# Hybrid decoder layer on one core: the whole value projection first, LRU gates and scans in the key and query steps

## The chip, the cores and the metric

The kernel runs on one core of one Trainium2 chip. The metric is the device time of one execution in microseconds, as a median of several runs. Engines are named as in the profile: PE is TensorE (PEld its weight loads), DVE is VectorE, ACT is ScalarE, POOL is GpSimd, SP is SyncE, which issues most of the DMAs.

## What is computed

One layer of a hybrid decoder on x of 256 tokens by 2048 channels, all in float32:

```python
u = rmsnorm(h, ln1_w)
proj = u @ w_in                      # six parts of 1024: lru_x, lru_g, q, k, v, ret_g
lru_x = causal_depthwise_conv(lru_x, conv_w, conv_b)
y_lru = rg_lru(lru_x, ...) * gelu(lru_g)        # two 128-wide gates per block, then a scan over the tokens
y_ret = retention(q, k, v, ret_g, gn_w)         # 8 heads, rotary, decay, group norm, swish gate
h = h + concat(y_lru, y_ret) @ w_out
u = rmsnorm(h, ln2_w)
h = h + (silu(u @ w_ffn_gate) * (u @ w_ffn_up)) @ w_ffn_down
return rmsnorm(h, final_norm_w)
```

The scale of the first rmsnorm is not applied to u. The kernel multiplies x by ln1_w alone and scales the results of the projections by 1/rms of the token; that factor comes from the sum of squares over all 2048 channels.

## The kernel before

**Precision.** Each float32 operand is split in two parts, a rounded high part h (a cast on ACT, L101) and the rest l (a subtraction on DVE, L102). A product is then three matmuls: h by h, h by l, l by h. Weights pass through the same split as they arrive: `Unit.load` (L111) takes 1024 columns of a weight into a `raw` buffer (five of them), casts into `wh` and subtracts into `wl` (four of each). In the value projection at the start this is done in two pieces of 512 columns.

**Order of the work.** All PE work is a list of steps, `program`. At the end of the function (L949 to L963) a loop goes through it: it issues the loads that a step needs and three more (`AHEAD = 3`), then the step's matmuls, and then calls `tick`, which runs what was put off with `defer(n, f)` n steps before. The order in which the program hands out instructions is their priority; a planner at compile time then fixes the order of each engine's queue and lets work whose operands are ready move ahead into gaps. At run time each queue is in order.

**Two kinds of step.** `fm_tile` (L165) gives a tile with the channels on partitions: 16 steps of k, each with one matmul of 512 columns (L140) and one of 256 (L141). `tm_block` (L180) gives a block with the tokens on partitions: four k's per weight unit, two token tiles, three matmuls of 512 columns (L156 to L158). A matmul of either kind fills a PSUM bank; there are four in the pool `bank` and four in `aux`. The `halfway` list is looked at in the middle of an `fm_tile`, at n == 8: there the norm's small products go in.

**The steps before the change.** First the left 512 columns of the value projection (`v0`, four steps), while x arrives (`load_x`, L858) and `make_u` (L275) turns it into u. `v0_out` (L870) copies the results out of PSUM unscaled, asks for the identity matrix and calls `squares` (L284): eight squares on ACT, the adds on POOL. The sum goes through `rms_scale` (L246): two small products on PE (L250), a reciprocal square root on DVE, two diagonal tiles (L254), and in the middle of the next tile a product that spreads it over the partitions (L260). `then` (L880) scales the two value tiles on POOL. Next are eight lru_x tiles (`lru_in` behind each: convolution on DVE), eight key tiles, eight query tiles (`qk_half`: rotary), the right 512 columns of the value projection (four steps), eight steps of the retention gate, which start with one head each (`head`), and eight lru gate tiles. Behind them come the output projection, the feed-forward part and the last norm, which the change doesn't touch.

The gates of the LRU (`lru_gate`, L354: six matmuls each), their roots (`lru_roots`, L370) and the scans (`lru_scan`, L375: a reciprocal, the scan instruction and six more on DVE, one square on ACT) are put off from the lru_x tiles. Before, the first four gates come behind the fourth key tile, the roots behind the first query tile, the scans from the third query tile to the seventh step of the retention gate. They have to be done when `lru_out` (L391) uses them.

Of the kernel before, what the change touches and what calls it, by code (L numbers as in the profile page):

```python
# [10 lines left out]
AF = mybir.ActivationFunctionType  # L11
ALU = mybir.AluOpType
# [24 lines left out]
def tile_hymba_layer(ctx: ExitStack, tc: tile.TileContext, A: dict, out: bass.AP):  # L37
# [21 lines left out]
    def act_tile(name, dt=F32):  # L59
        return apool.tile([P, 512], dt, tag="act", name=nm(name))  # L60
# [158 lines left out]
    def defer(steps, f):  # L219
        later.append([steps, f])  # L220
# [54 lines left out]
    def make_u(k):  # L275
        hl = act_tile("u", F32R)
        act.activation(out=hl[:, :S], in_=xs(k), func=AF.Copy, scale=col(C_LN1 + k))  # L277
        v.scalar_tensor_tensor(
            out=hl[:, S:], in0=xs(k), scalar=col(C_LN1 + k), in1=hl[:, :S].bitcast(F32),
            op0=ALU.mult, op1=ALU.subtract,  # L280
        )
        u[k] = hl

    def squares():  # L284
        for i in range(KT // 2):
            sq = act_tile("sq") if i else sumsq
            act.activation(out=sq, in_=xt[i], func=AF.Square)
            if i:
                pool.tensor_tensor(out=sumsq, in0=sumsq, in1=sq, op=ALU.add)
        pool.tensor_tensor(out=sumsq[:, :S], in0=sumsq[:, :S], in1=sumsq[:, S:], op=ALU.add)  # L290


    gw = [None] * 4
# [149 lines left out]
    def v_out(c, t, ps):  # L443
        vv[2 * t + c] = act_tile("v")
        act.activation(out=vv[2 * t + c], in_=ps, func=AF.Copy, scale=r1_tok[:, t : t + 1])
# [412 lines left out]
    def load_x(k):  # L858
        if k == 0:
            nc.sync.dma_start(out=small, in_=A["small"])  # L860
        if k < 2:
            nc.sync.dma_start(out=xt[0][:, k * S : k * S + S], in_=A["x"][0][:, k * S : k * S + S])
        elif k % 2 == 0:
            nc.sync.dma_start(out=xt[k // 2], in_=A["x"][k // 2])

    v0 = [
        Unit(A["w_v"][i], 2, lambda k, i=i: load_x(4 * i + k), lambda k, i=i: make_u(4 * i + k)) for i in range(4)
    ]

    def v0_out(t, ps, c0, cw):  # L870
        vv[2 * t] = act_tile("v")
        act.copy(out=vv[2 * t], in_=ps)
        if t == 0:
            return
        nc.sync.dma_start(out=ident, in_=A["ident"])
        squares()
        defer(2, load_gates)
        defer(3, lambda: halfway.append(lambda: rms_scale(sumsq[:, :S], r1_tok, r1, then)))

    def then():  # L880
        for t in range(2):
            pool.tensor_scalar(out=vv[2 * t], in0=vv[2 * t], scalar1=r1_tok[:, t : t + 1], scalar2=None, op0=ALU.mult)
        defer(2, lru_decay)
        trig[0] = act_tile("trig")
        nc.sync.dma_start(out=trig[0], in_=A["trig"])

    tm_block(v0, lambda k: u[k], v0_out)

    for n in range(NLRU):

        def post(ps, n=n):
            defer(max(1, 4 - n), lambda: lru_in(n, ps))
            defer(max(9, 12 - n), lambda: lru_gate(n))
            if n == NLRU - 1:
                defer(10, lru_roots)
                for m in range(NLRU):
                    defer((12, 15, 18, 20, 22, 24, 26, 28)[m], lambda m=m: lru_scan(m))

        fm_tile(Unit(A["w_lx"][n]), u, range(KT), post, room=aux if n in (2, 3, 6, 7) else bank)

    first = [True]
    for which in ("k", "q"):
        for j in range(4):
            for e in range(2):
# [7 lines left out]
                    qk_half(which, j, e, ps)  # L912

                fm_tile(Unit(A["w_" + which][2 * j + e]), u, range(KT), post)

    tm_block([Unit(A["w_v"][4 + i]) for i in range(4)], lambda k: u[k], lambda t, ps, c0, cw: v_out(1, t, ps))

    for c in range(2):

# [144 lines left out]
```

## Time and profile before

| | us |
|---|---|
| median of three runs | 1105.15 (1104.84 to 1106.02) |
| the profiled execution, its own time | 1106.04 |
| its span, first to last instruction | 1103.3 |
| PE busy | 1092.4 (99%) |
| DVE busy | 885.3 (80%) |
| ACT busy | 622.1 (56%) |
| POOL busy | 57.9 (5%) |

The profile is of one execution; its span leaves out what lies before the first instruction and behind the last. A row of a timeline gives the start, the time, engine, line, operation, tiles and count; with a count of two or more, the time is that of the group from its first start to its last end. Matmuls overlap: one of 512 columns has a length of 0.39 us, but the next one starts 0.23 us after it. The square bracket at the end says how long the engine was idle before and what ended that. A row of windows gives the stretch, its length and the busy time of each engine.

### The profile page before, as it was taken

How to read it: one execution, taken by the hardware profiler on the slowest of the kernel's cores; microseconds unless marked ns; L12 is line 12 of the kernel's file. 1: busy time of each engine (PE TensorE's matmuls, PEld its weight loads, DVE VectorE, ACT ScalarE, POOL GpSimd, SP SyncE). 2: the span in 40 equal slices, each digit the busy share in tenths (PEclk: the TensorE clock that was granted, in tenths of full speed). 3: DMA queues.
4: the chain of work that ended last, by engine and by line, in shares of the span. 5: the costliest groups of instructions: out<-in, count | busy, mean ns of one | idle time of the engine just before them, and what ended most of it. 6: DMA issues, size and time to landing. Idle time of an engine off the chain costs nothing.

```text
span 1103.3 us, 14624 instructions
## 1 busy us (share of the span) xinstructions
PE 1092.4 (99%) x5328; PEld 920.5 (83%) x5328; DVE 885.3 (80%) x1249; ACT 622.1 (56%) x846; POOL 57.9 (5%) x64
## 2 busy tenths in 40 slices
PE   9999999999999999999999999999999999999996
PEld 7888888888888988888888888888888888888885
DVE  7798799978776787788787878877887999777874
ACT  7666644468665665554554545544545675554552
POOL 0602130000000000000000000000000000020001
PEclk9999999999999999999999999999999999999999
DMA  9765575554665465645746646556456465646562
GB/s 329 239 199 168 171 245 170 176 188 143 194 220 187 155 207 174 213 154 186 247 132 214 226 156 229 187 191 219 159 195 234 153 219 196 224 161 218 201 230 76
DMA packets 62215, 214.71 MB, mean 195 GB/s; under 512 B 7104, under 2 KB 7488, under 8 KB 62144
## 3 DMA queue, kind: packets, MB, share of 16 engines
q1 hardware_dynamic: 61344, 211.70, 57.6%
q0 software_dynamic: 512, 1.57, 0.5%
q8 instruction: 41, 0.67, 0.3%
q10 hardware_dynamic: 288, 0.52, 0.1%
q14 instruction: 30, 0.25, 0.1%
HBM read 211.67 MB, written 2.10 MB: 194 GB/s over the span
## 4 chain that ended last, share of the span: by engine, by line
PE 98%; DVE 0%; DMA 0%; SPq 0%; ACT 0%; issue 0%; DVEq 0%
PE c L667 18%; PE c L669 18%; PE c L668 18%; PE fm L140 16%; PE fm L141 8%; PE p L667 3%; PE p L668 3%; PE p L669 3%; PE tm L156 3%; PE tm L157 3%; PE tm L158 3%; PE ft L719 1%; DMA x<-in_x 0%; PE fm L147 0%; PE fm L145 0%; PE fm L146 0%
## 5 line engine op out<-in xcount | busy, mean ns | idle before, releaser
L102 DVE TENSOR_TENSOR wl<-raw,wh 128x1024 fp32r<-128x1024 f32 (+1 forms) x364 | 438.0, 1216 | 150.5 <-ACT wh L101 146.2
L101 ACT CAST wh<-raw 128x1024 fp32r<-128x1024 f32 (+1 forms) x364 | 371.3, 1032 | 273.7 <-PE c L669 136.9
L668 PE MATMUL c<-wl,ah 128*128 128x512 f32 x848 | 326.4, 391 | 0.0
L669 PE MATMUL c<-wh,al 128*128 128x512 f32 x848 | 325.7, 390 | 0.0
L667 PE MATMUL c<-wh,ah 128*128 128x512 f32 x848 | 286.4, 390 | 0.0
L668 PEld LDWEIGHTS c<-wl,ah 128*128 128x128 f32 x848 | 159.2, 188 | 32.8
L669 PEld LDWEIGHTS c<-wh,al 128*128 128x128 f32 x848 | 159.2, 188 | 32.7
L667 PEld LDWEIGHTS c<-wh,ah 128*128 128x128 f32 x848 | 159.1, 188 | 32.6
L140 PE MATMUL fm<-u,wh 128*128 128x512 f32 x512 | 180.1, 396 | 0.0
L141 PE MATMUL fm<-u,wl 128*128 128x256 f32 x512 | 143.9, 281 | 0.0
L101 ACT CAST wh<-sum 128x1024 fp32r<-128x1024 f32 x64 | 66.9, 1053 | 87.0 <-PE c L669 40.2
L140 PEld LDWEIGHTS fm<-u,wh 128*128 128x128 f32 x512 | 96.0, 188 | 22.1
L141 PEld LDWEIGHTS fm<-u,wl 128*128 128x128 f32 x512 | 96.7, 189 | 0.2
L102 DVE TENSOR_TENSOR wl<-sum,wh 128x1024 fp32r<-128x1024 f32 x64 | 77.1, 1224 | 3.1 <-ACT wh L101 2.4
L140 PE MATMUL fm<-y,wh 128*128 128x512 f32 x224 | 78.8, 397 | 0.0
L141 PE MATMUL fm<-y,wl 128*128 128x256 f32 x224 | 62.5, 281 | 0.0
L823 POOL TENSOR_TENSOR htok<-htok,fw 128x512 f32<-128x512 f32 (+1 forms) x7 | 10.9, 1574 | 904.8 <-ACT junk L821 904.8
L140 PEld LDWEIGHTS fm<-y,wh 128*128 128x128 f32 x224 | 41.9, 188 | 10.2
L158 PE MATMUL tm<-wh,u 128*128 128x512 f32 x128 | 48.8, 390 | 0.0
L157 PE MATMUL tm<-wl,u 128*128 128x512 f32 x128 | 48.7, 392 | 0.0
L156 PE MATMUL tm<-wh,u 128*128 128x512 f32 x128 | 46.0, 396 | 0.9 <-ACT u L277 0.9
L141 PEld LDWEIGHTS fm<-y,wl 128*128 128x128 f32 x224 | 42.3, 189 | 0.2
(246 smaller groups left out, 1231.0 us busy)
## 6 DMA issues: line engine op xcount, KB each, us to landing
raw<-in_w_gu SPq DMA_DIRECT2D x176, 512.0 KB, 5.1
raw<-in_w_down SPq DMA_DIRECT2D x88, 512.0 KB, 4.4
raw<-in_w_out SPq DMA_DIRECT2D x32, 512.0 KB, 3.7
raw<-in_w_lx SPq DMA_DIRECT2D x16, 512.0 KB, 4.7
raw<-in_w_k SPq DMA_DIRECT2D x16, 512.0 KB, 4.0
raw<-in_w_q SPq DMA_DIRECT2D x16, 512.0 KB, 4.2
raw<-in_w_rg SPq DMA_DIRECT2D x16, 512.0 KB, 3.7
raw<-in_w_lg SPq DMA_DIRECT2D x16, 512.0 KB, 4.0
```

Source lines behind the costliest of these rows:

```text
L101: act.copy(out=dst_h, in_=src)
L102: v.tensor_tensor(out=dst_l, in0=src, in1=dst_h.bitcast(F32), op=ALU.subtract)
L140: pe.matmul(ps, wh, hl, start=first, stop=False)
L141: pe.matmul(ps[:, :S], wl, hl[:, :S], start=False, stop=last)
L156: pe.matmul(ps, ah, wh, start=first, stop=False)
L157: pe.matmul(ps, ah, wl, start=False, stop=False)
L158: pe.matmul(ps, al, wh, start=False, stop=last)
L667: pe.matmul(p, ah, bh, start=firsts[c] == m, stop=False)
L668: pe.matmul(p, ah, bl, start=False, stop=False)
L669: pe.matmul(p, al, bh, start=False, stop=last)
L719: pe.transpose(pt[:, o : o + P], g[:, (2 * b + c) * P : (2 * b + c) * P + P], ident)
L823: pool.tensor_tensor(out=h, in0=h, in1=fw[cb][:, c0 : c0 + cw], op=ALU.mult)
```

## The change

The value projection is done whole at the start: eight units of two k's and all 1024 columns, with four PSUM banks open at once. x arrives as before, but each x piece now stands behind the first weight piece of its k. The squares come with the loads, each added on DVE. The four value results stay in PSUM until the token's factor is known, and ACT scales them on the way out (`v_out`, L443). The second value block between queries and retention gate is gone. `lru_in` comes sooner behind its tile, the gates four steps sooner, the roots four steps sooner, and the scans between four and six steps sooner against their own tiles: now from the seventh key tile to the fifth step of the retention gate. The layout of w_v on the host changes to match.

```diff
-    def squares():
-        for i in range(KT // 2):
-            sq = act_tile("sq") if i else sumsq
-            act.activation(out=sq, in_=xt[i], func=AF.Square)
-            if i:
-                pool.tensor_tensor(out=sumsq, in0=sumsq, in1=sq, op=ALU.add)
-        pool.tensor_tensor(out=sumsq[:, :S], in0=sumsq[:, :S], in1=sumsq[:, S:], op=ALU.add)
+    def square(i):
+        sq = act_tile("sq") if i else sumsq
+        act.activation(out=sq, in_=xt[i], func=AF.Square)
+        if i:
+            v.tensor_tensor(out=sumsq, in0=sumsq, in1=sq, op=ALU.add)
...
-    v0 = [
-        Unit(A["w_v"][i], 2, lambda k, i=i: load_x(4 * i + k), lambda k, i=i: make_u(4 * i + k)) for i in range(4)
-    ]
-
-    def v0_out(t, ps, c0, cw):
-        vv[2 * t] = act_tile("v")
-        act.copy(out=vv[2 * t], in_=ps)
-        if t == 0:
-            return
-        nc.sync.dma_start(out=ident, in_=A["ident"])
-        squares()
-        defer(2, load_gates)
-        defer(3, lambda: halfway.append(lambda: rms_scale(sumsq[:, :S], r1_tok, r1, then)))
+        if k == KT - 2:
+            nc.sync.dma_start(out=ident, in_=A["ident"])
+
+    def before(m):
+        if m % 2 == 0:
+            load_x(m // 2)
+
+    def after(m):
+        k = m // 2
+        if m % 2 == 0:
+            make_u(k)
+        elif k % 2:
+            square(k // 2)
+
+    v_units = [Unit(A["w_v"][i], 2, lambda m, i=i: before(4 * i + m), lambda m, i=i: after(4 * i + m)) for i in range(KT // 2)]
+    v_ps = {}
+
+    def v_step(i):
+        def run():
+            for k in (2 * i, 2 * i + 1):
+                for c in range(2):
+                    for t in range(2):
+                        if k == 0:
+                            v_ps[t, c] = bank("v")
+                        wh, wl = v_units[i].part(2 * (k % 2) + c, 512, 0, 512)
+                        mm_tm(v_ps[t, c], u[k], t, wh, wl, k == 0, k == KT - 1)
+            if i == KT // 2 - 1:
+                v.tensor_tensor(out=sumsq[:, :S], in0=sumsq[:, :S], in1=sumsq[:, S:], op=ALU.add)
+                halfway.append(lambda: rms_scale(sumsq[:, :S], r1_tok, r1, then))
+                defer(2, load_gates)
+
+        return run
 
     def then():
-        for t in range(2):
-            pool.tensor_scalar(out=vv[2 * t], in0=vv[2 * t], scalar1=r1_tok[:, t : t + 1], scalar2=None, op0=ALU.mult)
+        for c in range(2):
+            for t in range(2):
+                v_out(c, t, v_ps[t, c])
         defer(2, lru_decay)
...
-    tm_block(v0, lambda k: u[k], v0_out)
+    for i in range(KT // 2):
+        program.append(([v_units[i]], v_step(i)))
...
-            defer(max(1, 4 - n), lambda: lru_in(n, ps))
-            defer(max(9, 12 - n), lambda: lru_gate(n))
+            defer(max(1, 2 - n), lambda: lru_in(n, ps))
+            defer(max(5, 8 - n), lambda: lru_gate(n))
             if n == NLRU - 1:
-                defer(10, lru_roots)
+                defer(6, lru_roots)
                 for m in range(NLRU):
-                    defer((12, 15, 18, 20, 22, 24, 26, 28)[m], lambda m=m: lru_scan(m))
-
-        fm_tile(Unit(A["w_lx"][n]), u, range(KT), post, room=aux if n in (2, 3, 6, 7) else bank)
+                    defer((8, 10, 12, 14, 16, 18, 20, 22)[m], lambda m=m: lru_scan(m))
+
+        fm_tile(Unit(A["w_lx"][n]), u, range(KT), post, room=aux if n in (0, 1, 4, 5) else bank)
...
-    tm_block([Unit(A["w_v"][4 + i]) for i in range(4)], lambda k: u[k], lambda t, ps, c0, cw: v_out(1, t, ps))
```

## Rows read from the trace of the kernel before

**Rows 1.** The page's first part: busy us (share of the span) and instructions of each engine

```profile
PE 1092.4 (99%) x5328; PEld 920.5 (83%) x5328; DVE 885.3 (80%) x1249; ACT 622.1 (56%) x846; POOL 57.9 (5%) x64
```

**Rows 2.** The waits of PE: who for whom, us in total, times, longest

```profile
PE tm L156 <- ACT u L277: 0.9, 1, 0.9
```

**Rows 3.** Windows by stage: first values; keys; queries; second values; retention gate with heads

```profile
4.92:28.50 23.58, 22.66 (x98) 18.21 (x98) 21.25 (x58) 19.00 (x35) 0.00 (x0) 1.00 1.00 364
...
75.50:122.50 47.00, 47.00 (x285) 41.78 (x284) 39.54 (x63) 29.72 (x51) 10.78 (x14) 1.00 0.52 172
122.50:169.80 47.30, 47.30 (x272) 41.14 (x271) 41.57 (x63) 24.04 (x34) 12.31 (x17) 1.00 0.64 212
169.80:191.90 22.10, 22.10 (x101) 18.35 (x100) 21.97 (x34) 9.86 (x13) 1.86 (x2) 1.00 0.57 179
191.90:242.50 50.60, 50.60 (x245) 42.68 (x244) 45.24 (x87) 29.17 (x46) 0.00 (x0) 1.00 0.56 182
```

**Rows 4.** The timeline of the first 13 us, all engines

```profile
2.57 0.43 SPq L862 DMA_DIRECT2D x<-in_x  x1
3.05 0.43 SPq L118 DMA_DIRECT2D raw<-in_w_v  x1
...
4.92 1.10 PE L156 MATMUL tm<-wh,u 128*128 128x512 f32 x2
...
5.82 0.62 ACT L101 CAST wh<-raw 128x512 fp32r<-128x512 f32 x1 [0.95 <-DMA raw<-in_w_v]
...
6.32 0.61 PE L158 MATMUL tm<-wh,u 128*128 128x512 f32 x2
6.47 0.69 DVE L102 TENSOR_TENSOR wl<-raw,wh 128x512 fp32r<-128x512 f32 x1 [0.85 <-ACT wh L101]
...
7.29 0.51 ACT L277 ACTIVATE u<-x,small 128x256 fp32r<-128x256 f32 x1 [0.86 <-DMA x<-in_x]
...
7.85 0.73 PE L156 MATMUL tm<-wh,u 128*128 128x512 f32 x2 [0.92 <-ACT u L277]
...
12.18 0.62 PE L156 MATMUL tm<-wh,u 128*128 128x512 f32 x2
```

**Rows 5.** A window of one microsecond in the start; the last number is GB/s

```profile
7.00:8.00 1.00, 0.15 (x1) 0.15 (x2) 0.40 (x3) 0.71 (x2) 0.00 (x0) 1.00 0.98 324
```

**Rows 6.** The timeline of PE in lru_x tiles, L140 three pairs apart, in two places

```profile
31.31 0.40 PE L140 MATMUL fm<-u,wh 128*128 128x512 f32 x1
...
32.37 0.40 PE L140 MATMUL fm<-u,wh 128*128 128x512 f32 x1
...
53.31 0.39 PE L140 MATMUL fm<-u,wh 128*128 128x512 f32 x1
...
54.35 0.39 PE L140 MATMUL fm<-u,wh 128*128 128x512 f32 x1
```

**Rows 7.** DVE's groups by line in the query stage: count, busy us, mean ns

```profile
L102 DVE TENSOR_TENSOR wl<-raw,wh 128x1024 fp32r<-128x1024 f32 x16 | 20.1, 1256 | 3.8 <-ACT wh L101 3.5
L380 DVE RECIPROCAL p<-p 128x256 f32<-128x256 f32 x2 | 3.5, 1744 | 0.0
...
L387 DVE TENSOR_TENSOR_SCAN hs<-a,b 128x256 f32<-128x256 f32 x1 | 1.2, 1228 | 0.0
...
L385 DVE TENSOR_TENSOR b<-b,p 128x256 f32<-128x256 f32 x2 | 0.8, 419 | 0.0
```

**Rows 8.** The timelines of POOL and of DVE behind the first value block

```profile
29.93 12.56 POOL L289 TENSOR_TENSOR sumsq<-sumsq,sq 128x512 f32<-128x512 f32 x7 [29.07 <-ACT sq L287]
...
33.94 5.70 DVE L102 TENSOR_TENSOR wl<-raw,wh 128x1024 fp32r<-128x1024 f32 x3 [5.57 <-ACT wh L101]
```

**Rows 9.** The timelines of PE and of DVE around the norm's products

```profile
44.25 0.58 PE L250 MATMUL rms<-ones,sumsq 128*128 128x2 f32 x4
...
48.56 0.92 DVE L254 TENSOR_SCALAR diag<-ident,r_tok 128x128 f32<-128x128 f32 x2
```

**Rows 10.** The waits of ACT from the keys to the end of the retention gate

```profile
ACT wh L101 <- PE fm L140: 30.9, 22, 1.8
```

More of the change, by code (lines that the diff above doesn't have):

```diff
@@ L1033 @@
         "w_k": _fm(seg[3][:, rope], np),
-        "w_v": _tm(seg[4], np),
+        "w_v": seg[4].reshape(KT // 2, 2, P, 1024).transpose(0, 2, 1, 3).reshape(KT // 2, P, 2048),
         "w_rg": _tm(seg[5], np),
```

## The prediction

> **What bounds the kernel now.** I read the page's busy times first, then the waits of PE, then the windows by stage, then the first 13 us instruction by instruction. PE is busy in 99% of the span [rows 1], so a gain has to come from PE's few idle places or from PE's pace. The list of PE's waits has one entry after the warm-up: 0.9 us at the start of the first value projection, for a u tile [rows 2]. From there on the windows show PE busy in every microsecond up to the last stage: 47.00 of 47.00 in the key stage, 47.30 of 47.30 in the query stage, 22.10 of 22.10 in the second value block, 50.60 of 50.60 in the gate stage with the heads [rows 3]. All of these stages are limited by the number of matmuls. The tail after the last matmul belongs to lines the change doesn't touch, so what the change can give lies ahead of about 12 us, and what it can cost lies where DVE is almost as full as PE: 21.97 of 22.10 us in the second value block, 45.24 of 50.60 behind it [rows 3].
>
> **The matmuls.** They are neither more nor fewer. Before, each half of the value projection has 16 steps of k with 2 token tiles and 3 products: 96 matmuls of 512 columns. After, there are 16 steps with 2 halves, 2 tiles and 3 products: 192. Gates, heads, norms and the other tiles issue what they issued. Removed from PE's path: 0; added: 0.
>
> **The start.** Here PE waits for data. The first matmul starts at 4.92, the six of k = 0 occupy PE until about 6.77 (two of L158 from 6.32 on, 0.227 us apart), and the next start is at 7.85 [rows 4]. It waits for ACT's u of k = 1, which itself waited 0.86 us for the second half of the first x tile [rows 4]. Four steps, 24 matmuls, are behind PE at 12.18 [rows 4]. At 0.227 us each (the 0.62 us of a row of two is one start-to-start step of 0.227 and one full length of 0.39) 24 take 5.45 us; 12.18 - 4.92 - 5.45 = 1.81 us are lost after the first matmul. No change of this kind can win more than that here.
>
> After the change the second group of six needs only the other 512 columns of the same k and no x. Those stand in the second weight piece, cast at 5.82 to 6.44 and split by DVE until 7.16 [rows 4]; the products with wh start at 6.77 and those with wl at 6.77 + 2 x 0.227 = 7.22, just in time. So PE works through to 6.77 + 1.36 = 8.13. For k = 1 it needs x's second half, which now has three weight pieces ahead of it instead of two: it is asked for at 3.05 instead of 2.57 [rows 4], behind 256 KB more. At the 324 GB/s of that microsecond [rows 5] these are 0.81 us, and the least is nothing, since the later piece already shared the queue. Nearest to it is the request's own delay, 0.48, and I take 0.65, between the two: PE starts on k = 1 at 7.85 + 0.65 = 8.5, and 24 matmuls are done at 8.5 + 12 x 0.227 = 11.22 instead of 12.18. That is **-0.96 us**; with no delay it is -1.33 (PE is then limited by its own 8.13), with the whole 0.81 it is -0.80, and with twice that, 1.62, it would be 0. Behind it a k takes PE 2.72 us and asks for 256 + 256 + 128 KB, 241 GB/s, under the 324 that the queue moves early on, so there is no second wait.
>
> **Squares, and sums moved from POOL to DVE.** Seven adds of 512 and one of 256 were on POOL, 12.56 us for the seven [rows 8]. On DVE they lie in the value stage. DVE is there busy 21.25 of 23.58 us [rows 3] for half the weights and all of u, some 8 us of which are small instructions pulled forward and u; the other half of the weights adds 16 splits of 0.69 [rows 4], 11.0 us, the adds at most 8 x 0.69 = 5.5: 37.8 us in a stage of 192 x 0.227 = 43.5 us. PE covers it: cost 0. Were the cover gone it would be the 5.5. Against this stands what POOL's adds did to DVE: three weight splits took 5.70 us beside them, 1.9 each [rows 8], where 1.25 is usual [rows 7], 2 us in these three alone. The Trainium skill ("Perfetto Trace Analysis", Optimizing Scalar/DVE Operations) says that if DVE is saturated, offloading to Scalar or GPSIMD may make sense, which speaks against this move; by it DVE would be 5.5 us fuller, and the time longer by what of them PE doesn't cover, at most all: 1104.3 + 5.5 = 1109.8; by the rows it is 0. The same section warns that the two share a read port, and the stretched splits agree with that.
>
> **The values kept in PSUM.** Four banks hold them until r1_tok is known. The norm's two small products come in the middle of the first lru_x tile, the diagonal for the spread was done 5.2 us after them (44.25 to 49.48) [rows 9], and the next middle is about 5.9 us later: unhidden cost 0, bound +1 us if DVE is later than it was. The four scaled copies out of PSUM have until the third lru_x tile asks for a bank, half a tile (2.7 us) behind the spread, and need only one of the four by then; ACT has 1.25 us casts to fit between. I take 0, bound +1.
>
> **DMAs and queues.** ident is requested with the last x instead of behind the value block, 15 us and more ahead of its use; gates and trig stay behind their own steps on SP. Nothing waits for them on PE: 0.
>
> **Gates, roots and scans.** The gates' 48 matmuls stay, in earlier places. The scans lose the second value block as a place to hide: keys to end of the gate stage shrink from 167.0 to 145.2 us (96 x 0.227 = 21.8 less), DVE's work there from 39.54 + 41.57 + 21.97 + 45.24 = 148.3 to 138.3, eight splits of 1.25 fewer [rows 3, 7]. Its share goes from 89% to 95%: full, but not over. In the query stage alone four scans fall due instead of the two whose reciprocals stand there [rows 7]; a scan is 1.74 + 1.23 at most + six near 0.42 = 5.5, so 41.57 + 2 x 5.5 = 52.6 us of work meet 47.3: 5.3 over. What hides it: ACT waits 22 times, 30.9 us together, for PE to give back a split buffer [rows 10], so the weights are up to three buffers of 2.8 us, 8.4 us, ahead. 5.3 is less: cost 0, and the gate stage then has room again.
>
> **PE's pace between two patterns.** A pair of L140 and L141 does not always take the same time: three pairs take 1.06 us at 31.31 and 1.04 at 53.31 [rows 6], 6.7 ns a pair, with no wait. The slower pattern stands from the first lru_x tile to the norm's products, 2.75 tiles, and from the first gates, behind the fourth key tile, to the last query, 12 tiles, together 14.75 x 16 = 236 pairs; the faster one in between. If norm and gates set it again, after the change half an lru_x tile and all keys and queries are slow, 264 pairs: **+0.2 us**.
>
> **Sum.** -0.96 + 0.2 = -0.8 us. The profiled execution took 1106.04 us for a span of 1103.3, 2.7 around it; the median of the runs shown is 1105.15, 0.9 lower. I carry the difference over: 1105.15 - 0.8 = 1104.35, said as **1104.3**.
>
> **The rivals.**
> *DVE becomes the bound in the queries.* If the static order places the scans ahead of the weight splits, the 5.3 us of excess come out at PE, in the last query tiles and the first gate steps. For it: 95% load, and DVE full already behind the queries. Against: 8.4 us of lead, and that PE did not wait once at 99% DVE. It decides from the point where the backlog passes the lead. Wholly exposed it gives 1104.35 + 5.3 = 1109.7, and **slower**; exposed for 3 us, 1107.4. Chance 0.13.
> *The start gives nothing.* The x tile comes later by 1.62 us or more, and PE waits as before: 1105.15 + 0.2 = 1105.4. For it: early transfers are uneven. Against: the next pieces came soon behind. Chance 0.15.
> *The fast pattern takes keys and queries.* All but 8 of the 236 slow pairs turn fast: 228 x 6.7 ns = 1.5 us, and 1105.15 - 0.96 - 1.5 = 1102.7, **faster**. For it: what flips the pattern isn't known. Against: all five gate insertions went into the slow one. Chance 0.09. All slow from the start would add 120 pairs, 0.8 us: 1104.35 + 0.8 = 1105.2, chance 0.07.
> *The forecast* keeps 0.56.
>
> **The numbers.** A change of 0.2% (2.2 us) is about the least that a measurement of this kernel can tell from none. Faster: 0.09, the fast pattern alone. Slower: 0.13, the DVE rival. Same: 0.78. Likeliest time 1104.3. The range goes from 1102.7, the fast pattern, to 1107.2, the DVE rival a little exposed with the start's gain gone as its neighbour; left out are most of the DVE rival and little else.
>
> **What would show it.** Right: the wait for u near 7 us shrinks from 0.9 to under 0.5, PE's 24th matmul starts at about 11; keys and queries show 1.06 us for three pairs; no further wait in PE's list. Wrong: waits of PE for wl, sc or a bank between 140 and 235 us, or a wait at the rms spread; a start at which k = 1 still begins after 9.5.

## The result and the profile after

The median went from 1105.03 (12 runs, 1104.75 to 1106.02) to **1107.68 us** (12 runs, 1106.87 to 1109.61): a ratio of 1.0026 [1.0017, 1.0035]. The forecast was 1104.3, its range 1102.7 to 1107.2. The change makes the kernel slower, and the time lies above the range.

Part 1 of the page answers to [rows 1]: PE has 0.9 us more, DVE 1.6, POOL 15.1 less.

```profile
PE 1093.3 (99%) x5328; PEld 920.0 (83%) x5328; DVE 886.9 (80%) x1265; ACT 620.7 (56%) x854; POOL 42.8 (4%) x54
```

The waits of PE after (engine, line, who it waited for: us in total, times, longest), against [rows 2]:

```profile
PE tm L157 <- DVE wl L102: 1.6, 3, 0.7
PE warm L94 <- DVE eps_t L87: 1.0, 1, 1.0
PE v L156 <- ACT wh L101: 0.8, 1, 0.8
```

The wait for u at the start has become one of 0.8 us for a weight. The first line is new: three waits for split weights, all in the retention gate. The windows after, for the value projection, the keys, the queries, and the retention gate with the heads (PE, PEld, DVE, ACT, POOL), answer to [rows 3]:

```profile
4.99:49.98 44.99, 44.22 (x193) 36.00 (x193) 37.94 (x85) 32.47 (x61) 0.00 (x0) 1.00 0.91 321
97.00:145.00 48.00, 48.00 (x284) 42.19 (x284) 36.44 (x57) 32.31 (x57) 12.18 (x14) 1.00 0.49 158
145.00:192.10 47.10, 47.10 (x269) 40.84 (x267) 46.76 (x71) 20.01 (x27) 12.65 (x16) 1.00 0.61 201
192.10:242.30 50.20, 48.60 (x224) 39.65 (x223) 48.13 (x83) 23.14 (x32) 2.46 (x2) 1.00 0.59 189
```

DVE is full in queries and gate stage (46.76 of 47.10, 48.13 of 50.20), while in the keys 11.6 us of it are free. Over the three stages it is busy 131.3 of 145.3 us, 90%. The share over the whole hid the two full stages.

**Where the 2.4 us are** (last matmul at 1094.06 before, 1096.45 after). Start: PE's first lru_x matmul comes at 49.98; before, at 28.50, and the 96 matmuls of the other half, at 0.227 us each, took 21.77 us later on, so 50.27: -0.29. lru_x, keys and queries: +0.8, of which 0.2 are PE's pairs and 0.6 are products of the first head that now stand ahead of the stage's end. From the value block on: +1.9 with those 0.6 gone from it, so about 2.5. The list counts 1.6 for the three waits, but from start to start the two steps around each are 0.97, 0.48 and 0.97 us longer than the usual 0.227 each, 2.4 together: they are the loss.

The medians differ by 2.65 us. Their spans, listed with every run, differ by 2.1 to 2.2 (1103.2 to 1103.4 before, 1105.45 after); the rest lies outside the span, where all kernels with the new start spend 1.93 to 2.26 us in the median and all with the old one 1.77 to 1.81. What that is, no run shows.

The first of the three waits, on DVE (start, us, line, operation, tiles):

```profile
192.58 1.22 DVE L102 TENSOR_TENSOR wl<-raw,wh 128x1024 fp32r<-128x1024 f32 x1
...
194.39 0.68 DVE L385 TENSOR_TENSOR_SCAN hs<-a,b 128x256 f32<-128x256 f32 x1
194.98 1.72 DVE L378 RECIPROCAL p<-p 128x256 f32<-128x256 f32 x1
196.72 0.85 DVE L438 TENSOR_TENSOR rope<-qk,n 64x256 f32<-64x256 f32 x2
197.60 1.23 DVE L102 TENSOR_TENSOR wl<-raw,wh 128x1024 fp32r<-128x1024 f32 x1
```

The cast of that weight on ACT:

```profile
189.41 1.06 ACT L101 CAST wh<-raw 128x1024 fp32r<-128x1024 f32 x1 [1.54 <-PE fm L140]
```

And PE, which needs it next:

```profile
197.58 0.61 PE L156 MATMUL tm<-wh,u 128*128 128x512 f32 x2
198.89 0.50 PE L157 MATMUL tm<-wl,u 128*128 128x512 f32 x1 [0.69 <-DVE wl L102]
199.23 0.40 PE L158 MATMUL tm<-wh,u 128*128 128x512 f32 x1
```

The cast was done at 190.47, 7.1 us ahead of PE's first use of it (197.58) and 8.4 ahead of the use of the split. The split stood behind scan, reciprocal and rotary work in DVE's queue and was done at 198.83, on the spot. DVE's finished splits were 4 to 10 us ahead of PE in the lru_x tiles and keys, 1 to 4 from 160 to 184, and 0.1 to 1.5 us from 187 to 228. The first and the last split of the query stage, each with PE's first use of it:

```profile
139.43 1.21 DVE L102 TENSOR_TENSOR wl<-raw,wh 128x1024 fp32r<-128x1024 f32 x1
...
146.43 0.28 PE L141 MATMUL fm<-u,wl 128*128 128x256 f32 x1
...
187.20 1.22 DVE L102 TENSOR_TENSOR wl<-raw,wh 128x1024 fp32r<-128x1024 f32 x1
...
189.56 0.28 PE L141 MATMUL fm<-u,wl 128*128 128x256 f32 x1
```

The lead shrinks from 5.8 to 1.1 us, so the queries use up 4.7 us of it without a wait. In the kernel before it is 6.1 us at the first of them, never under 4.0, and 6.3 at the last.

### The profile page after: what moved, and what is told of

Read it like the earlier page. It is cut to its first block, busy times and chain, and to the rows that moved or that the text cites. A ratio compares the mean times of both kernels' runs of the same rounds, so it can differ in the third digit from the quotient of the medians.

```text
span 1105.6 us, 14656 instructions
## 1 busy us (share of the span) xinstructions
PE 1093.3 (99%) x5328; PEld 920.0 (83%) x5328; DVE 886.9 (80%) x1265; ACT 620.7 (56%) x854; POOL 42.8 (4%) x54
## 4 chain that ended last, share of the span: by engine, by line
PE 93%; DVE 5%; issue 1%; DMA 0%; ACT 0%; SPq 0%; DVEq 0%
PE c L666 18%; PE c L665 18%; PE c L667 18%; PE fm L140 14%; PE fm L141 7%; PE p L667 3%; PE p L665 3%; PE p L666 3%; PE v L157 1%; PE v L156 1%; PE v L158 1%; DVE wl L102 1%; PE ft L717 1%; DVE p L378 1%; PE tm L157 1%
## 5 line engine op out<-in xcount | busy, mean ns | idle before, releaser
L140 PE MATMUL fm<-u,wh 128*128 128x512 f32 x512 | 180.5, 397 | 0.0
L140 PEld LDWEIGHTS fm<-u,wh 128*128 128x128 f32 x512 | 96.2, 188 | 22.2
L140 PE MATMUL fm<-y,wh 128*128 128x512 f32 x224 | 79.0, 399 | 0.0
L140 PEld LDWEIGHTS fm<-y,wh 128*128 128x128 f32 x224 | 42.0, 188 | 10.3 <-DVE y L102 0.2
L666 PE MATMUL p<-wl,sh 128*128 128x512 f32 x96 | 37.4, 389 | 0.0
L667 PE MATMUL p<-wh,sl 128*128 128x512 f32 x96 | 37.3, 390 | 0.0
L626 DVE TENSOR_TENSOR sum<-raw 128x512 f32<-128x512 f32 x32 | 22.0, 687 | 17.2 <-DMA raw<-in_w_gu 15.0
```

The source lines that it names most:

```text
L140: pe.matmul(ps, wh, hl, start=first, stop=False)
L626: v.tensor_tensor(out=t1, in0=b11, in1=b12, op=ALU.add)
L666: pe.matmul(p, ah, bl, start=False, stop=False)
L667: pe.matmul(p, al, bh, start=False, stop=last)
```

## The experiments

Each run stands beside runs of the kernel before on the same chip (their medians lie between 1105.03 and 1105.46). Diffs are against the kernel after where nothing else is said.

### Is it DVE?

**no_recip** leaves the scan's reciprocals out (p is used without its inversion).

```diff
-        v.reciprocal(out=p, in_=p)
```

> The changed kernel without the reciprocals of the scans: eight instructions of 1.74 us on DVE are left out, 13.9 us, nearly all between the queries and the retention gate; PE's instructions stay. Theory DVE: no wait of PE for wl, time 1105.2 to 1105.6 (the changed kernel less 2.1 to 2.4). Rival ORDER (PE waits for something that the planner's order sets, not for DVE's fill): waits of 1 us or more remain, time over 1106.5. Rival PATTERN: 1107.7.

1104.33 us (1103.78 to 1105.63), 0.9995 [0.9986, 1.0004]. That is below the band that theory DVE gave. With the reciprocals gone (8 of 1.74 us; DVE's busy time is 12.5 us lower) all waits behind the start are gone; PE's list holds the start alone:

```profile
PE v L156 <- ACT u L277: 1.3, 1, 1.3
PE warm L94 <- DVE eps_t L87: 1.0, 1, 1.0
```

**scans_late** gives gates, roots and scans the distances that they had before, with the new start.

```diff
-            defer(max(5, 8 - n), lambda: lru_gate(n))
+            defer(max(9, 12 - n), lambda: lru_gate(n))
...
-                defer(6, lru_roots)
+                defer(10, lru_roots)
...
-                    defer((8, 10, 12, 14, 16, 18, 20, 22)[m], ...
+                    defer((12, 15, 18, 20, 22, 24, 26, 28)[m], ...
```

> The changed kernel, with gates, roots and scans put off by as many steps as before the change: only the value projection has moved. Theory DVE (the scans and the rotary work of the queries overfill DVE, and the weight splits come late): two scans instead of four fall into the queries, so the four late splits and the 2.1 us that PE waited between 197 and 224 us go or shrink below 0.5 us; time about 1105.2, that is 2.4 less than the changed kernel's 1107.7 and level with before. Rival BLOCK (the second value block was the only room for DVE, so that without it DVE is too full wherever the scans stand): waits of PE for wl of 1.5 us or more remain, in the retention gate or among the lru gates; time 1106.5 to 1108. Rival PATTERN (the loss is PE's slower pattern): no change, 1107.7.

1111.37, 1.0059 [1.0046, 1.0071], above all three expectations. PE's waits moved behind the gate stage, to the start of the output projection:

```profile
PE yt L503 <- DVE o L495: 2.1, 2, 1.3
PE fm L140 <- DVE y L102: 1.5, 1, 1.5
```

Four windows there (after PE and the other engines' busy times: granted clock, DMA share, GB/s):

```profile
290.00:294.00 4.00, 2.89 (x18) 2.27 (x16) 3.13 (x6) 3.23 (x7) 0.00 (x0) 1.00 0.50 175
294.00:298.00 4.00, 1.77 (x8) 1.14 (x8) 3.12 (x9) 3.27 (x11) 0.00 (x0) 0.66 0.39 134
298.00:302.00 4.00, 3.69 (x11) 2.99 (x12) 3.97 (x12) 2.51 (x9) 0.00 (x0) 0.50 0.00 0
302.00:306.00 4.00, 4.00 (x24) 3.45 (x23) 1.85 (x6) 2.09 (x4) 0.00 (x0) 0.98 0.09 29
```

PE is busy 2.89 and 1.77 of 4 us, the granted clock falls to 0.50, the lower of its two levels (1.2 of 2.4 GHz), and waits of 3.6 us cost some 6 in the median. Without the second value block the scans can't go back to their old places.

**v_late** is the kernel before with only the distances of gates, roots and scans taken from after: both value blocks stay.

> The kernel before, with only the gates, roots and scans moved to the places of the changed kernel; both value blocks stay where they were. Theory DVE: four scans in the queries overfill DVE here too, but the value block behind them takes up the backlog, in four steps that have no work of their own for DVE but the splits; PE waits under 0.5 us, time 1105.0 plus or minus 0.5. Rival QUERIES (the overload in the queries alone does it): PE waits 1 us or more near the end of the queries, time 1106 to 1107.5.

1109.39, 1.0038 [1.0026, 1.0051]. This is above both expectations, and the value block did not take up the backlog. The waits are like those of after, two in the second value block (ended at 177.5 and 189.0) and one at the start of the gate stage (198.7):

```profile
PE tm L157 <- DVE wl L102: 1.8, 3, 0.9
```

So the earlier, denser scans cost by themselves, with the value block still there and the start of the kernel before.

### Is it the places or the load?

**spread** brings gates and roots two steps forward and draws the scans apart.

```diff
-            defer(max(5, 8 - n), lambda: lru_gate(n))
+            defer(max(3, 6 - n), lambda: lru_gate(n))
...
+                defer(4, lru_roots)
...
+                    defer((5, 7, 10, 13, 16, 19, 21, 24)[m], ...
```

> The changed kernel with its DVE work spread by what each stage has free: gates and roots two steps sooner, the scans from the fourth key step to the seventh step of the retention gate, mostly three steps apart instead of two. Nothing is taken away. Theory FILL (PE waits only where DVE's work falls due faster than DVE does it, since the windows leave DVE 11.6 of 48 us in the keys, next to nothing in queries and retention gate, 6.8 of 48 among the lru gates): no wait of PE for wl or o over 0.4 us, time 1105.2 to 1105.6. Rival TOTAL (without the second value block DVE has too little room from queries to lru gates as a whole): waits of 1.5 us or more remain somewhere, time over 1106.7.

1106.53, 1.0013 [1.0004, 1.0021], between the two expectations. About half of the loss comes back, and the waits for weights are gone; one is left, for a head's scores:

```profile
PE pv L465 <- DVE sc L459: 1.3, 1, 1.3
```

**two_roots** brings the gates two steps forward, splits the roots in two batches, and the first scans come in the middle of the keys (steps behind the fourth and the eighth lru_x tile).

```diff
...
-                    defer((8, 10, 12, 14, 16, 18, 20, 22)[m], ...
+                    defer(((5, 6, 9, 12), (10, 13, 16, 22))[half][m], ...
```

> The changed kernel with the roots taken in two batches, so that four scans are due from the last lru_x tile to the sixth key tile, in room that DVE has there (10 us of 47 free among the lru_x tiles), and the other four three or more steps apart from the first query tile to the fifth step of the retention gate. Nothing is left out. Theory FILL: the one wait that was left when the scans were merely spread (1.3 us for a head's scores) goes, no wait of PE for DVE over 0.4 us, time 1104.9 to 1105.4. Rival TOTAL: a wait of over 1 us stays at another place, time 1106 or more.

1109.16, 1.0033 [1.002, 1.0045]. The scans fill DVE earlier; the waits, ended between 196 and 210 us, stay. DVE is busy 45.46 of 48.00 us in the keys and 46.56 of 47.00 in the queries, and only 41.90 of the 50.00 us behind them, but there it is full until 220: the splits' lead is 3.4 us where the queries begin and 0.1 at 152. The free time of a stage as a whole did not help; it came behind the splits that were late.

**spread_b** lies between the two: spread with (5, 6, 8, 11, 14, 17, 21, 24).

> The kernel after with the gates of the later tiles two steps sooner, the roots after four steps and the scans after 5, 6, 8, 11, 14, 17, 21 and 24: between the even placing of spread (1106.53 us) and the dense one of two_roots (1109.16). Theory PLACE (PE's waits come from more scans in a stretch than DVE's free time there, so they depend on where the scans stand): the two scans brought into the last key tiles, where spread left DVE at 42 of 48 us, empty the query stage, spread's one wait of 1.3 us near 208 goes, and the time is 1105.3 to 1106.3. Rival TOTAL (between keys and the end of the gate stage DVE is simply too full, wherever the scans stand): a wait of about 1 us moves to the keys and the time stays at 1106.5 to 1107.5.

1107.5, 1.0023 [1.0014, 1.0032]. The time is at the upper edge of TOTAL's band, but both theories missed on the wait: it neither went nor moved to the keys. PE waits once, 2.0 us, until 208.3, and DVE's timeline shows what stands ahead of that split:

```profile
202.84 1.74 DVE L378 RECIPROCAL p<-p 128x256 f32<-128x256 f32 x1
...
205.11 1.74 DVE L378 RECIPROCAL p<-p 128x256 f32<-128x256 f32 x1
206.77 0.36 DVE L433 TENSOR_TENSOR qk<-qk,cr 128x256 f32<-128x256 f32 x1
207.05 1.21 DVE L102 TENSOR_TENSOR wl<-raw,wh 128x1024 fp32r<-128x1024 f32 x1
```

Two scans that were asked for four steps apart (17 and 21) stand side by side. The distance sets the order in which the planner hears of work, not the time at which it runs, so moving a scan by a step or two shifts the pile-up in ways that these numbers don't foretell.

**fewer** settles the load with the whole layer computed: with q = 1/(1+t) the decay is 2q - 1, on ACT, and b is 2 q s iu. The correction of the root's rounding, (s*s + t) in place of 2t, is left out.

```diff
-        v.scalar_tensor_tensor(out=p, in0=t, scalar=1.0, in1=s, op0=ALU.add, op1=ALU.mult)
+        v.tensor_scalar(out=p, in0=t, scalar1=1.0, scalar2=None, op0=ALU.add)
         v.reciprocal(out=p, in_=p)
-        v.scalar_tensor_tensor(out=a, in0=t, scalar=1.0, in1=s, op0=ALU.subtract, op1=ALU.mult)
-        v.scalar_tensor_tensor(out=a, in0=a, scalar=-1.0, in1=p, op0=ALU.mult, op1=ALU.mult)
-        act.activation(out=b, in_=s, func=AF.Square)
-        v.tensor_tensor(out=b, in0=b, in1=t, op=ALU.add)
-        v.tensor_tensor(out=b, in0=b, in1=p, op=ALU.mult)
+        act.activation(out=a, in_=p, func=AF.Identity, scale=2.0, bias=neg1)
+        v.scalar_tensor_tensor(out=b, in0=p, scalar=2.0, in1=s, op0=ALU.mult, op1=ALU.mult)
```

> The kernel after with a shorter scan. With q = 1/(1+t) the decay is a = 2q - 1 (on ACT) and b = 2 q s iu: five instructions on DVE (0.38 + 1.74 + 0.42 + 0.48 + 0.75 us) in place of eight (5.33 us), 1.56 us less a scan, 12.5 us in all, between keys and the gate stage. What is left out is the correction of the root's rounding, (s*s + t) in place of 2t. Theory LOAD (PE waits because DVE's work between 97 and 243 us is too much for the time there; no_recip took away 13.9 us and stood at 1104.33): no wait above 0.5 us behind the start, and 1104.0 to 1104.8 us. Rival PLACE (the order of the scans among the splits alone makes the waits): a wait near 200 us stays, 1105.5 to 1107.

1104.94 (1104.53 to 1105.33), 0.9995 [0.9986, 1.0004]: 2.7 us below after, a little above the expected band; DVE's whole busy time fell by 9.5 us (886.9 to 877.4), not 12.5. PE waits for nothing behind the start. Its queries and its gate stage:

```profile
145.00:192.00 47.00, 47.00 (x268) 40.79 (x267) 46.35 (x69) 21.10 (x29) 15.09 (x16) 1.00 0.64 211
192.00:242.00 50.00, 50.00 (x242) 42.18 (x241) 42.96 (x81) 28.24 (x46) 1.74 (x2) 1.00 0.54 172
```

The queries' DVE is as busy as in after, and PE has no wait in either stage. A full DVE is not the harm as long as its splits keep a lead: here it is 1.8 us or more in the queries, 4.2 at their end (1.1 in after), and the gate stage behind has room. What no run tried is to put the splits ahead of the scans in DVE's queue with all of the work kept, or to give them more buffers.

**before_fewer** gives the kernel before the same scan.

> The kernel before with the shorter scan: the control for fewer. Its DVE was never late, so theory LOAD expects no gain: 1105.0 to 1105.5, and fewer stands 0.5 to 1.2 us below it, which is then what the new order at the start is worth without DVE's waits. Rival (a lighter DVE helps any order): 1104.3 or less, and fewer not below it.

1104.76 (1104.55 to 1105.66), 0.9994 [0.9985, 1.0003]; lower than expected, though not to be told from before. fewer stands 0.2 us above it, not 0.5 to 1.2 below: with DVE's waits taken out of both, the new order is worth nothing that these runs can tell. (Inside the span fewer's median is 0.1 us shorter, 1102.9 against 1103.0; outside it is 0.3 longer.)

### Does POOL help?

**pool_b** gives three of a scan's eight instructions (L382 to L384) to POOL.

```diff
-        v.tensor_tensor(out=b, in0=b, in1=t, op=ALU.add)
+        pool.tensor_tensor(out=b, in0=b, in1=t, op=ALU.add)
...
```

> The changed kernel with three of the eight DVE instructions of each scan (an add and two multiplications, 0.42 us each, 10 us in all) on POOL instead. The Trainium skill (Perfetto Trace Analysis, Optimizing Scalar/DVE Operations) says both that offloading may make sense when DVE is saturated and that the shared port may make it useless. Theory OFFLOAD: DVE is relieved by up to 10 us, PE's waits for wl go below 0.7 us in all, time 1105.3 to 1106.0. Rival PORT: the DVE instructions beside POOL's get longer by as much as DVE was relieved (in the kernel before, three splits beside POOL's adds took 1.9 us each instead of 1.25), the waits stay at 1.5 us or more, time 1107.3 to 1108.5.

1114.51, 1.0087 [1.0073, 1.01], the slowest of all, and far above PORT's band. Its waits of PE, and the windows of queries and gate stage:

```profile
PE tm L157 <- DVE wl L102: 3.6, 3, 2.7
PE fm L141 <- DVE wl L102: 2.4, 1, 2.4
```

```profile
145.00:192.10 47.10, 44.59 (x244) 38.06 (x244) 46.13 (x59) 18.87 (x26) 25.14 (x27) 0.97 0.56 191
192.10:242.30 50.20, 46.56 (x222) 38.20 (x222) 48.09 (x70) 21.77 (x31) 15.94 (x15) 0.99 0.50 168
```

DVE does 129 instructions where it did 154 (24 went to POOL), in the same time (94.2 and 94.9 us): beside POOL many of the rest take longer, a split 1.38 us where it was 1.28, one of 256 columns on the queries' qk tiles 0.60 where it was 0.41; the reciprocals stay at 1.74. Part of the loss is TensorE's clock: behind the wait of 2.4 us (ended at 189.2) the granted clock stands at its lower level.

```profile
190.00:192.00 2.00, 2.00 (x8) 1.71 (x8) 2.00 (x4) 0.00 (x0) 0.79 (x1) 0.50 0.82 266
```

**squares_pool** puts the adds of the squares back on POOL (in `square` and behind the last step).

```diff
-            v.tensor_tensor(out=sumsq, in0=sumsq, in1=sq, op=ALU.add)
+            pool.tensor_tensor(out=sumsq, in0=sumsq, in1=sq, op=ALU.add)
```

> The changed kernel with the adds of the squares back on POOL, the squares still spread among the loads. Theory HIDDEN (DVE has room in the value stage, so it doesn't matter who adds): time 1107.7 within 0.4, the waits of the start and of the retention gate as they were. Rival ADDS (the adds on DVE delay the weight splits of the value stage): the first lru_x matmul starts over 0.4 us sooner and the time is 1107.2 or less. Rival PORT: DVE's splits beside POOL's adds take 1.3 times as long or more and the start gets longer, 1108.2 or more.

1110.6, 1.0046 [1.0033, 1.0058]. The first lru_x matmul starts at 53.05 where it was 49.98, and PE's list has a line more:

```profile
PE v L157 <- DVE wl L102: 1.6, 2, 1.4
```

DVE's splits and u tiles of this stage (count, busy us, mean ns); in after they take 687 and 476 ns:

```profile
L102 DVE TENSOR_TENSOR wl<-raw,wh 128x512 fp32r<-128x512 f32 x31 | 20.1, 680 | 1.9 <-ACT wh L101 1.9
L278 DVE SCALAR_TENSOR_TENSOR u<-x,small,u 128x256 fp32r<-128x256 f32 x16 | 9.0, 601 | 0.3 <-ACT u L277 0.3
```

So the start gets longer, as rival PORT said, but not through longer splits: the u tiles and the small lam instructions (0.43 us where they took 0.16) lengthen, and a split comes late behind them. The adds on DVE are worth 3 us within the new order. The Trainium skill ("Perfetto Trace Analysis", Optimizing Scalar/DVE Operations) says that offloading to Scalar or GPSIMD may make sense when DVE is saturated; for POOL, pool_b speaks against it here (in squares_pool DVE had room: 37.94 of 44.99 us with the adds on it). Its warning in the same section, that the two share a read port, agrees with the longer instructions in both runs, which don't show the port itself.

### The start

**x_sooner** asks for x's second half ahead of the third weight piece; **act_queue** lets ACT issue the first x tiles.

```diff
-        if m % 2 == 0:
+        if m == 1:
+            load_x(1)
+        elif m % 2 == 0 and m != 2:
             load_x(m // 2)
```

```diff
-            nc.sync.dma_start(out=xt[0][:, k * S : k * S + S], ...
+            act.dma_start(out=xt[0][:, k * S : k * S + S], ...
```

x_sooner:

> The changed kernel with x's second half asked for one place sooner, ahead of the third weight piece, as the kernel before had it. Theory QUEUE (the second weight piece landed at 6.72 instead of 5.79 because the large piece behind it shared the DMA engines; x's half behind it takes less): it lands near 5.8, the second group of six starts at 6.7 to 6.9 instead of 7.41, the start is 0.4 to 0.6 us shorter and the time is 1107.1 to 1107.3. Rival CHANCE (landing times at the start scatter by a microsecond from run to run): the second piece lands at 6.3 or later, time 1107.7 within 0.3.

act_queue:

> The changed kernel with the small tile and the two halves of the first x tile asked for by ACT instead of SP, so that the second weight piece is asked for at about 1.2 us instead of 2.1. Theory REQUEST (the start is set by when a piece is asked for): the second piece lands at 5.8 or sooner, PE begins the second group without its wait of 0.8 us, the first lru_x matmul starts at 49.2 to 49.5 instead of 50.0, time 1106.9 to 1107.2. Rival RATE (the first 12 matmuls wait for some 700 KB, and the queue moves 260 GB/s whatever is asked for when): first lru_x matmul at 49.8 or later, time within 0.3 of 1107.7.

x_sooner: 1107.57, 1.0023 [1.0013, 1.0033], first lru_x matmul at 49.86; after: 1107.68 and 49.98. act_queue: 1108.47, 1.0034 [1.0022, 1.0046]; PE waits 1.8 us for u and lru_x starts at 50.74. Neither order made the start measurably shorter: whatever came first, something else was late. In after it was the second weight piece (start, us, engine, line, tiles):

```profile
6.74 1.23 ACT L101 CAST wh<-raw 128x512 fp32r<-128x512 f32 x2 [1.81 <-DMA raw<-in_w_v]
...
7.41 0.73 PE L156 MATMUL v<-wh,u 128*128 128x512 f32 x2 [0.77 <-ACT wh L101]
...
8.14 0.50 PE L157 MATMUL v<-wl,u 128*128 128x512 f32 x1
```

The same cast began at 5.82 before [rows 4].

### PE's pace

After the gates a pair of 512 and 256 columns takes 353 ns, as before, and 347 in most of lru_x. **nudge** puts two matmuls of 2 columns behind each gate, between two pairs; **mid_nudge** puts two inside a pair, once behind the last gates of the keys (129 us) and once in the output projection (296 us).

```diff
         pe.matmul(ps, wh, hl, start=first, stop=False)
+        if between and not first:
+            between.pop()()
...
```

nudge:

> The changed kernel with two more matmuls of 2 columns behind the gates of each block (eight places, five in PE's order, some 0.1 to 0.4 us each), of the same form as the norm's products, behind which the fast pattern stood in every trace so far. Theory RESET (what PE does just ahead sets whether three pairs take 1.06 or 1.04 us): keys and queries run in the fast pattern, 250 pairs gain 6.7 ns each, 1.7 us, less the matmuls' own 0.4 to 2: time 1106.4 to 1107.7. Rival SPLITS (the pattern hangs on where weights or results lie, not on what ran ahead): the pairs behind the gates stay at 1.06 us for three, and the time is 1107.9 to 1109.5. PE's waits in the retention gate are the same or longer under both, since PE reaches them sooner.

mid_nudge:

> The changed kernel with two added matmuls of 2 columns put between the matmul of 512 and that of 256 columns of one pair, once behind the last gates among the keys and once in the output projection; the norm's products, which stood ahead of the fast pattern, were between such a pair as well, while the added matmuls that changed nothing stood between two pairs. Theory INSIDE (a push inside a pair sets the pattern): three pairs take 1.04 us behind each, 190 pairs of keys and queries and some 180 of the output projection gain 6.7 ns, 2.5 us, for 0.9: time 1106.0 to 1106.5, less if the waits shrink. Rival NONE: the pairs stay at 1.06 for three, time 1108.3 to 1109.

nudge: 1111.3, 1.0059 [1.0046, 1.0072]: behind none of its eight insertions, the last at 127 us, does the pace change (it stays at 353 ns until 179 and then turns fast with nothing inserted there), and they cost about 0.45 us each. mid_nudge: 1106.87, 1.0013 [1.0004, 1.0022]. PE around the insertion:

```profile
127.97 0.40 PE L147 MATMUL fm<-u,wh 128*128 128x512 f32 x1
...
129.03 0.39 PE L147 MATMUL fm<-u,wh 128*128 128x512 f32 x1
129.26 0.50 PE L143 MATMUL nudge<-ones 128*128 128x2 f32 x4
129.62 0.37 PE L150 MATMUL fm<-u,wl 128*128 128x256 f32 x1
...
130.18 0.39 PE L147 MATMUL fm<-u,wh 128*128 128x512 f32 x1
...
131.22 0.39 PE L147 MATMUL fm<-u,wh 128*128 128x512 f32 x1
```

Three pairs take 1.06 us ahead of it and 1.04 behind it, and so on to 185 us, where PE waits 0.8 us for a weight: keys and queries take 94.4 us where after takes 94.0, so here DVE's lateness and the insertion eat the whole gain. What is left comes from the second insertion, behind which the output projection runs fast throughout; from its start to the last matmul of the kernel PE takes 1.0 us less than in after. In the middle of it:

```profile
339.94 0.39 PE L147 MATMUL fm<-y,wh 128*128 128x512 f32 x1
...
340.98 0.40 PE L147 MATMUL fm<-y,wh 128*128 128x512 f32 x1
```

In the median mid_nudge is 0.8 us below after.

**before_mid**, **spread_mid**, **fewer_mid** and **two_mid** try the same two insertions in the kernels before, spread_b, fewer and two_roots.

before_mid:

> The kernel before with two matmuls of 2 columns inside a pair, once behind the last of the four gates that follow the fourth key tile and once in the output projection; nothing else changes. Theory INSIDE (a push inside a pair flips the pattern, a push between pairs doesn't): some 190 pairs in keys and queries and 250 in the output projection and the feed-forward part's start take 346.7 instead of 352.5 ns, 5.8 ns x 440 = 2.5 us, less 2 x 0.45 us for the nudges: about 1103.5 us, or 0.9985 of before. As DVE has its lead in this kernel, the gain should reach the time in full. Rival EATEN (the faster matmuls are lost again as waits for wl, as in mid_nudge): waits appear in the queries and the time is 1104.5 to 1105.5. Rival NONE: 1106.

spread_mid:

> spread_b with the two pushes of before_mid. Theory INSIDE with PLACE: spread_b's time less 1.2 to 1.6 us, about 1104.5, and no wait above 0.5 us in keys and queries. Rival EATEN: the faster PE meets DVE's fill, a wait for wl of about 1 us appears between 180 and 210 us, and the time is within 0.5 us of spread_b's.

fewer_mid:

> fewer with mid_nudge's two pushes, behind the last gates and in the output projection. With DVE's room regained the faster pairs of the queries (some 55 us, 150 pairs of 6.5 ns, 1.0 us) and, where the second push holds, of the output projection (250 pairs of 5.8 ns, 1.4 us) come through whole, less 0.9 for the pushes: fewer's time less 0.1 where only the first holds, less 1.5 where both do, about 1103. Rival EATEN: a wait for wl takes it back, and the time is fewer's.

two_mid:

> The roots in two batches and the two pushes inside a pair together. Theories FILL and INSIDE: no wait of PE over 0.4 us behind the start and the fast pattern in keys, queries and output projection, time 1103.2 to 1103.9, faster than the kernel before. FILL alone: 1105.6 to 1106.4. INSIDE alone: 1105 to 1105.5.

before_mid: 1105.22, ratio 1.0 [0.9991, 1.0009]. The queries turn fast (346.7 ns, some 125 pairs, 0.8 us), the output projection doesn't stay so, and two insertions cost 0.9: nothing is left. spread_mid: 1108.5, 1.0034 [1.0021, 1.0046]; the pace in keys and queries is that of spread_b. fewer_mid: 1105.84, 1.0005 [0.9996, 1.0013]; it stays at 353, and the median is fewer's plus 0.9, the price of the insertions. two_mid: 1109.68, 1.0038 [1.0025, 1.005]; the pace is 346.7 from 131 to 160, and PE waits 1.7 us for a weight. So the first insertion inside a pair flipped the pace in three of these five kernels, the second in one (mid_nudge): that the place decides has fallen as a rule, and what does stays open.

None of the runs stands measurably below the kernel before; of those that compute the whole layer, fewer and before_fewer come nearest.

## Why the prediction was wrong

**The failed step** is in the part on gates, roots and scans: "the weights are up to three buffers of 2.8 us, 8.4 us, ahead. 5.3 is less: cost 0, and the gate stage then has room again." The 8.4 us were read from ACT's waits [rows 10], and ACT's casts do run nearly as far ahead (7.3 us in most of the queries, 7.1 at the first wait). But PE needs DVE's split too, and that has no such lead: it stands in DVE's queue where the planner put it, behind scans whose turn came first. The lead to compare with the excess was the split's, 4 to 6 us at the start of the queries. The excess itself was sized well: 5.3 us forecast, and 4.7 us of lead used up in the queries, which the split's lead just covered. But the gate stage then had no room to win it back: DVE is busy 48.13 of 50.20 us there, the lead stays near nothing, and each late split comes out at PE. The term set at 0 measured about 2.4 us. A DVE that is 99% full without a wait [rows 3, second value block] was taken as a sign of safety; the stage behind it still had 5.4 us free.

**The sum of DVE's work** was right enough: 138.3 of 145.2 us forecast, 131.3 of 145.3 found. The share of 95%, "full, but not over", judged three stages together; in the keys 11.6 us stay free, since scans need the roots, and they were of no use to the stages behind.

**The rival that came** is "DVE becomes the bound in the queries", given 0.13, priced at 5.3 us wholly exposed and 1107.4 at 3 us; about 2.5 came out. no_recip and fewer show it from the side of the load, v_late from that of the places. Its mechanism, scans placed ahead of splits, was as described, its place only in part: no wait stands in "the last query tiles", all three are in the gate stage, ended 6.8, 18.2 and 31.5 us into it.

**The start** was forecast at -0.96 and gave -0.29 at PE's first lru_x matmul. The wait for x's second half did shrink, as forecast; but the step "cast at 5.82" was carried over from before as if landings were fixed, and here it was 6.74. PE's 24th matmul behind the first started at 11.90, not 11.22. In the eighteen other profiles it lies anywhere from 11.3 to 13.6, so one profile's landing times are no term of a sum to 0.1 us. The first lru_x matmul starts at 49.96 in the median of the thirteen profiles with this start unaltered, and at 50.36 in that of the four with the old one (the 21.77 added): about -0.4. "The start gives nothing" had 0.15; it was nearer than -0.96, though its reason, that PE waits for x as before, did not come.

**Squares** were right: DVE had room for them (37.94 of 44.99 us, 37.8 forecast), and the one wait of the value stage, for the second weight piece, has nothing to do with them. **PE's pace** was right: +0.2 forecast, 0.2 found, keys and queries all slow. **Values in PSUM, ident, gates' DMAs**: no wait in PE's list, as forecast.

## What to carry to other kernels

Where an operand passes two engines, the lead that counts is that of the last one: take it from the end of its instruction to the start of the consumer, tile by tile, and not from waits on the first. Judge a full engine stage by stage, and ask whether there is room for what spills over before the lead is used up. An order that frees an early microsecond and concentrates side work later can be dearer than what it frees; cutting the side work itself (9.5 us less on DVE) brought back all that the placing had cost.

## What was not expected

The start can run at half the pace for some microseconds. In before_mid's profile PE stands idle 0.60 us between its warm-up and the first product, and what follows runs at half the pace until 9.9 us, two matmuls of 512 columns in 1.05 us where 0.62 is usual:

```profile
5.85 1.22 PE L165 MATMUL tm<-wh,u 128*128 128x512 f32 x2 [0.60 <-ACT u L286]
6.87 1.05 PE L166 MATMUL tm<-wl,u 128*128 128x512 f32 x2
...
10.11 0.62 PE L167 MATMUL tm<-wh,u 128*128 128x512 f32 x2
```

The windows print a granted clock of 1.00 there, but they take 1.00 wherever nothing is recorded, and this trace's record of the full clock begins only at 9.88 us. The same stands in spread_mid and fewer_mid, where it begins at 9.78 and 9.50; in the other seventeen profiles it begins between 3.9 and 7.2. The idle time alone doesn't decide it: act_queue's PE was idle for 1.82 us and no_recip's for 1.30 at the same place, and their first products run at the full pace (record from 5.77 and 4.36). What does stays open.

before_mid's first lru_x matmul comes at 29.62 instead of 28.50. The times of these three profiled executions are the longest of their own runs; the medians hold less of it. That it makes up the scatter of 1 to 2 us between executions of one kernel is likely, but was only argued. And POOL: its work beside a busy DVE cost more than it took away, in both places where it was tried.
